# RWKV-7 mixer in a two-layer trunk: the inverse of the chunk matrices changes layout by VectorE block transposes instead of DRAM round trips, with a new order of products

## The chip, the cores and the metric

One core of one Trainium2 chip runs the whole kernel. The metric is the device time of one execution in microseconds; lower is better. The median of 3 runs of the kernel before is 1144.75 us (1141.47 to 1145.14). The core's engines are named as in the profile: PE (TensorE, with PEld for its weight loads), DVE (VectorE), ACT (ScalarE), POOL (GpSimd) and SP (SyncE, which here issues most DMAs). Everything is float32 or float32 split into two parts.

## The reference, cut to what matters

Two layers of a post-norm trunk at 256 tokens and width 1024. Each layer is SwiGLU, a mixer, SwiGLU, each followed by a layer norm. Layer 0's mixer is a chunked spatial gate; layer 1's is RWKV-7 time mixing with 16 heads of 64, and the change is in this mixer alone.

```
def step(state, inp):
    r_t, w_t, k_t, v_t, a_t, b_t = inp
    sa = jnp.einsum('bhij,bhj->bhi', state, a_t)
    state = (state * w_t[:, :, None, :] + sa[..., None] * b_t[:, :, None, :]
             + v_t[..., None] * k_t[:, :, None, :])
    y = jnp.einsum('bhij,bhj->bhi', state, r_t)
    return state, y
```

After the scan, y is normalised per head, a bonus `sum(r*k*r_k) * v` is added, the result is multiplied by a gate g and by the matrix w_o.

## The kernel before, in words

**Stages.** The 256 tokens are two row blocks of 128 (m = 0, 1), each of two chunks of 64 tokens (ch = 0 to 3). Weights stream from HBM as tiles of 128x1024 (`raw`, 4 buffers); most are split into a high part by ScalarE (line 118) and a low part by VectorE (line 119), and every product is then three matmuls (`mm3`, lines 219 to 224). R and V are multiplied natively in float32 (line 301). RWKV's scan is done in chunk form. With decays folded in (`Ep`, `Em`, and `Ex`, which is `Ep` shifted down by a row, lines 803 to 823), each chunk needs masked products of keys with queries: `ab` (line 977, the strictly lower part that must be inverted) and `scores` (`sc`, line 1003). The vectors of a chunk that replace the recurrence come from the inverse of a unit triangular 64x64 matrix for each of 16 heads and 4 chunks.

**The inverse.** Each 64x64 matrix is cut into 32x32 blocks. The 128 diagonal blocks are inverted at once on VectorE, one block per partition, its 1024 elements along the free axis: 31 steps `i0` to `i30` (line 1027), two VectorE instructions each, the second waiting for the first. To get from "row of a block per partition" to "one block per partition", `ab` stores its masked tiles to DRAM (`dA`, line 999, issued by POOL) and `inv_load` reads them back (line 1023, issued by ScalarE). On the way out `inv_out` (line 1044) stores H and a transposed copy to DRAM (`dH`, `dG`) and reads them back in two layouts, `G` and `Hf`, all issued by SP. `offdiag` (`od`) and `offdiag2` (`oe`) then make the off-diagonal block with small 32x32 matmuls, and `Hf[m]` is the finished inverse that `u` multiplies.

**The chain of chunks.** `Chunk` (line 1106) has for each chunk `av`, `x`, `rs`, `u`, `s`, `y`. `u` needs `Hf` and X; `s` needs u's result in `VU` and the gathered keys `KB` (line 885, DMAs issued by POOL); `x`, `rs` of the next chunk need the state from `s`; `y` needs `VU` and the scores. The last steps are the normalisation `on`, `og` on VectorE, the transposition `oc` and the product with w_o (`O`).

**What sets the order.** PE's and SP's instructions run in program order. For the mixer that is the string `ORDER` (line 1389), one token per step: `K h m i`, `R h m i` and `V h m i` are half-products (half h of the columns, row block m, half i of the contraction; the second half ends with `kdone`, `rdone` or `vdone`, lines 836, 899, 912), `cZ`, `cB`, `cR`, `cK` are transpositions, `lw`, `la`, `dec`, `l1_` the small low-rank products, `g1`, `g2`, `ga` the gate, `dc` the shifted Ex (line 815), `dw` the chunk decays (line 825), `p:` a parameter load. DVE, ACT and POOL are ordered by the compiler's scheduler, within the data dependences; once compiled, each runs its list in that order. Tiles named `s4` share 22 SBUF buffers, `s4x` 12, PSUM has 2 banks `mm`, 2 `tp` and 4 `acc`; a tile whose buffer is still read makes its writer wait. Weight loads are issued ahead by SP in the same queue as the other SP transfers.

**R.** `rdone` reads R's PSUM bank twice on VectorE (lines 906, 907), for R with its decay and for the bonus.

Of the kernel before, what the change touches and what calls it, by code (L numbers as in the profile page):

```python
# [22 lines left out]
P = 128  # L23
D = 1024
# [113 lines left out]
class Builder:  # L138
# [529 lines left out]
    def rwkv(self, S):  # L668

        nc = self.nc  # L670
        a = {k[5:]: v for k, v in self.a.items() if k.startswith("rwkv_")}
        V, G, A = nc.vector, nc.gpsimd, nc.scalar
        mm = nc.tensor.matmul
# [84 lines left out]
        def mix(n, m, q, out):  # L758
            for k in range(4 * q, 4 * q + 4):
                s = slice(k * P, k * P + P)  # L760
                V.scalar_tensor_tensor(out[:, s], st["xx"][m][:, s], st["mu"][:, n * 8 + k:n * 8 + k + 1],
                                       st["xf"][m][:, s], op0=ALU.mult, op1=ALU.add)
# [209 lines left out]
        def masked(out, ps, mask):  # L972
            n = mask.shape[1]
            V.tensor_tensor(out.rearrange("p (h t) -> p h t", t=n), ps.rearrange("p (h t) -> p h t", t=n),
                            mask.unsqueeze(1).broadcast_to([P, 512 // n, n]), op=ALU.mult)

        def ab(m, c):
            def f():
                if c == 0:
                    st["Aab", m] = self.s4("Aab")  # L980
                t = st["Aab", m]
# [10 lines left out]
                if c == 0:  # L992
                    return
                t3 = t.rearrange("p (b z) -> p b z", z=64)
                for blk in range(2):
                    for e in range(2):
                        b0 = blk * 64 + e * 32 + m * 16
                        r0 = e * 64 + blk * 32
# [24 lines left out]
        def inv_load():  # L1023
            st["M"] = self.s4("M")
            DI.dma_start(st["M"], self.dA.rearrange("b s t -> b (s t)"))

        def inv_step(s):
            def f():
                if s == 0:
                    st["T1"] = self.small("T1", [P, 256])  # L1030
                M3, H3 = (st[k].rearrange("p (s t) -> p s t", s=32) for k in "MH")
                n = 31 - s
                hv, tv = H3[:, 0:s + 1, s + 1:32], st["T1"][:, :(s + 1) * n].rearrange("p (s t) -> p s t", t=n)
                V.tensor_tensor(tv, H3[:, 0:s + 1, s:s + 1].broadcast_to([P, s + 1, n]),
                                M3[:, s:s + 1, s + 1:32].broadcast_to([P, s + 1, n]), op=ALU.mult)
                V.tensor_tensor(hv, hv, tv, op=ALU.add)
            return f

        def inv_zero():
            st["Hf"] = [self.s4("Hf", x=True) for m in range(2)]  # L1040
            for t in st["Hf"]:
                V.memset(t, 0.0)

        def inv_out():
            Mt, Ht = st["M"], st["H"]
            M3, H3 = (t.rearrange("p (s t) -> p s t", s=32) for t in (Mt, Ht))
            q = DO
            q.dma_start(self.dH.rearrange("b s t -> b (s t)"), Ht)
            V.tensor_copy(M3[0:64], H3[0:64].rearrange("p s t -> p t s"))
            Hf = st["Hf"]  # L1050
            q.dma_start(self.dG.rearrange("b s t -> b (s t)"), Mt[0:64, :])
            Gt = self.s4("G")
            st["G"] = Gt

            def back(m, blk, e):
                b0 = blk * 64 + e * 32 + m * 16
                r0 = e * 64 + blk * 32
                q.dma_start(
                    Hf[m].rearrange("p (b t) -> p b t", t=64)[r0:r0 + 32, :, blk * 32:blk * 32 + 32],
                    self.dH[b0:b0 + 16].rearrange("b s t -> s b t"))  # L1060

            for e in range(2):
                q.dma_start(Gt.rearrange("p (b t) -> p b t", t=32)[e * 64:e * 64 + 32],
                            self.dG[e * 32:e * 32 + 32].rearrange("b s t -> s b t"))
            for m in range(2):
                for blk in range(2):
# [200 lines left out]
        DX, DW, DA, DI, DO = A, nc.sync, G, A, nc.sync  # L1267
# [23 lines left out]
        for m in range(2):  # L1291
            ops.update({f"l1_{m}": lora1(m), f"dc{m}": decay_x(m), f"dw{m}": decay_w(m), f"kb{m}": kb(m), f"st{m}": stash(m),
                        f"un{m}": unstash(m), f"g1_{m}": lora_g1(m), f"ln{m}": ln(m), f"od{m}": offdiag(m),
                        f"oe{m}": offdiag2(m)})
            for i in range(2):
                t = f"{m}{i}"
                for n, c in ((0, "R"), (1, "K"), (2, "V"), (5, "G")):
# [3 lines left out]
                    "dec" + t: decay(m, i), "kp" + t: kprep(m, i), "zb" + t: zb(m, i), "kn" + t: kn(m, i),  # L1301
# [35 lines left out]
def body(tc, nc, stages, **a):  # L1337
    with contextlib.ExitStack() as es:
# [51 lines left out]
p:k_k cm00 cm01 l1_0 lw00 mixK00 flush mixK01 K000 K001 cm10 cm11 la00 lw01 dec00 p:k_a dec01 dc0 mixK10 p:gn_g  # L1390
l1_1 mixV00 la01 la10 lw10 mixK11 K010 kp00 K011 lw11 zb00 kp10 K100 K101 kp01 dec10 zb01 cZ00 K110 hz cB00 dw0
dec11 dc1 K111 zb10 la11 kp11 mixV01 V000 kn10 cB10 mixR00 mixG00 cB01 mixR01 V001 g1 zb11 ih kn11 kn00 cZ01 p:r_k
ab00 R000 mixG01 cZ10 R001 cZ11 cB11 ab01 cR00 mixR10 V100 ab10 ab11 iload i0 g1_0 mixG10 R100 i1 i2 i3 R101 dw1
mixV10 p:gn_b kn01 i4 cR01 i5 st0 mixG11 mixV11 V010 cK00 sc000 V011 i6 i7 i8 rs0 i9 kb1 g2 cK10 cK11 i10 i11 V101
g1_1 cK01 i12 i13 i14 sc001 V110 i15 sc010 i16 kb0 V111 i17 mixR11 i18 i19 i20 i21 i22 i23 i24 i25 st1 vu00 sc011
i26 i27 ga00 i28 i29 av0 vu01 x0 i30 iout R010 od0 od1 oe0 bo00 oe1 bo01 u0 gb R011 s0 R110 cR10 av1 vu10 x1 R111
u1 rs1 ga01 s1 cR11 sc100 y0 vu11 sc101 y1 av2 sc110 x2 rs2 u2 sc111 un0 on00 on01 og00 y2 bo10 s2 av3 ga10 og01 x3
# [21 lines left out]
```

## Time and profile before

| | before |
|---|---|
| median of 3 runs | 1144.75 us |
| the profiled execution | 1143.73 us, span 1142.0 us |
| instructions | 15347 |
| mean granted PE clock | 0.988 |
| busy share of the span: PE, PEld, DVE, ACT, POOL | 97%, 77%, 61%, 42%, 4% |
| DMA, mean over the span | 190 GB/s |
| RWKV mixer | about 724.9 to 945.7 us of the span |

Times in rows are microseconds from the span's start. A row of the timeline gives start, duration, engine, line, operation, output and inputs, and in brackets the idle time of that engine just before it with what ended it. An engine name with q (SPq, ACTq) is its queue, which issues DMAs. [...] PE's matmuls are pipelined, so a busy PE is not necessarily PE at its peak.

### The profile page before, as it was taken

Reading aid. Unit: us, or ns where it says so; the run is one execution under the profiler, and the core shown is the slowest. Engines: PE = TensorE matmul, PEld = TensorE weight load, DVE = VectorE, ACT = ScalarE, POOL = GpSimd, SP = SyncE. Lnnn points to the kernel's source line nnn. Section 1 sums busy time; section 2 is a strip of 40 time slices with the busy share of each in tenths; the row PEclk is TensorE's granted clock in tenths of the full one; section 3 lists DMA queues with packets and bytes.
Section 4 is the critical chain, followed back from the end, with each engine's and each line's share of the span. In section 5 each row is a group of like instructions: output and inputs, shape, how many; then the busy total and the mean of one; then the engine's idle time right before and its main releaser. Section 6 shows DMA issues by size and latency. Waiting matters only on the chain.

```text
span 1142.0 us, 15347 instructions
## 1 busy us (share of the span) xinstructions
PE 1103.9 (97%) x5860; PEld 879.1 (77%) x5860; DVE 698.7 (61%) x969; ACT 480.5 (42%) x636; POOL 42.2 (4%) x44
## 2 busy tenths in 40 slices
PE   8999999999999999999999999999989889999997
PEld 5888888778888788888888888775555668788885
DVE  6654556769658555457655453878655787555544
ACT  5544443455335444444444452462123245444430
POOL 0000000100000000000000000112100110000000
PEclk9999999999999999999999999999999989999999
DMA  8776565775645766655677563437876146766530
GB/s 289 236 235 185 185 197 168 232 268 196 208 148 155 240 206 198 186 183 157 197 221 225 183 202 124 166 93 256 271 203 237 43 129 191 239 204 196 184 111 38
DMA packets 153933, 216.51 MB, mean 190 GB/s; under 512 B 21213, under 2 KB 114845, under 8 KB 153858
## 3 DMA queue, kind: packets, MB, share of 16 engines
q1 hardware_dynamic: 152394, 210.80, 57.7%
q0 software_dynamic: 1024, 3.15, 1.0%
q10 hardware_dynamic: 440, 1.57, 0.4%
q8 instruction: 46, 0.75, 0.3%
q14 instruction: 29, 0.24, 0.1%
HBM read 209.46 MB, written 3.42 MB: 186 GB/s over the span
## 4 chain that ended last, share of the span: by engine, by line
PE 81%; DVE 7%; DMA 5%; issue 2%; ACT 2%; POOL 1%; ACTq 0%; SPq 0%; DVEq 0%; POOLq 0%
PE mm L221 15%; PE mm L223 15%; PE mm L222 15%; PE acc L221 8%; PE acc L222 8%; PE acc L223 8%; PE mm L301 3%; DMA raw<-ffn_w_in 2%; DVE wl L119 2%; PE tp L415 2%; POOL rs L259 1%; PE tp L235 1%; ACT wh L118 1%; DMA raw<-rwkv_w_rkv 1%; PE tp L577 1%
## 5 line engine op out<-in xcount | busy, mean ns | idle before, releaser
L119 DVE TENSOR_TENSOR wl<-raw,wh 128x1024 fp32r<-128x1024 f32 (+1 forms) x332 | 396.2, 1209 | 267.1 <-ACT wh L118 259.8
L118 ACT CAST wh<-raw 128x1024 fp32r<-128x1024 f32 (+1 forms) x332 | 340.3, 1041 | 340.8 <-PE acc L223 146.0
L221 PE MATMUL mm<-wh,xh 128*128 128x512 f32 x832 | 327.3, 393 | 5.5 <-ACT wh L118 2.4
L222 PE MATMUL mm<-wl,xh 128*128 128x512 f32 x832 | 324.7, 390 | 0.6 <-DVE wl L119 0.6
L223 PE MATMUL mm<-wh,xl 128*128 128x512 f32 x832 | 325.1, 391 | 0.2 <-DVE xl L228 0.2
L221 PEld LDWEIGHTS mm<-wh,xh 128*128 128x128 f32 x832 | 156.5, 188 | 41.5 <-ACT wh L118 3.9
L223 PEld LDWEIGHTS mm<-wh,xl 128*128 128x128 f32 x832 | 156.6, 188 | 34.6 <-DVE xl L228 1.9
L222 PEld LDWEIGHTS mm<-wl,xh 128*128 128x128 f32 x832 | 156.7, 188 | 33.1 <-DVE wl L119 1.3
L221 PE MATMUL acc<-wh,hT 128*128 128x512 f32 x352 | 141.4, 402 | 0.0
L222 PE MATMUL acc<-wl,hT 128*128 128x512 f32 x352 | 137.4, 390 | 0.0
L223 PE MATMUL acc<-wh,hT 128*128 128x512 f32 x352 | 137.4, 390 | 0.0
L404 ACT ACTIVATE h<-mm 128x256 f32<-128x256 f32 x88 | 33.8, 384 | 106.0 <-PE mm L223 105.9
L223 PEld LDWEIGHTS acc<-wh,hT 128*128 128x128 f32 x352 | 66.1, 188 | 14.8
L222 PEld LDWEIGHTS acc<-wl,hT 128*128 128x128 f32 x352 | 66.2, 188 | 12.6
L221 PEld LDWEIGHTS acc<-wh,hT 128*128 128x128 f32 x352 | 66.1, 188 | 12.7
L405 DVE TENSOR_TENSOR h<-h,mm 128x256 f32<-128x256 f32 x88 | 36.8, 418 | 59.8 <-ACT h L404 59.8
L301 PE MATMUL mm<-raw,mix 128*128 128x512 f32 x128 | 59.4, 609 | 0.9 <-DMA raw<-rwkv_w_rkv 0.9
L259 POOL TENSOR_TENSOR rs<-ve,mhalf 128x1 f32<-128x1 f32 x14 | 14.2, 1011 | 926.2 <-DVE ve L267 926.2
L301 PEld LDWEIGHTS mm<-raw,mix 128*128 128x128 f32 x128 | 23.6, 193 | 26.6 <-issue 23.8
L228 DVE TENSOR_TENSOR hT<-tp,hT 128x512 fp32r<-128x512 f32 x44 | 30.2, 686 | 7.6 <-ACT hT L227 7.6
L227 ACT CAST hT<-tp 128x512 fp32r<-128x512 f32 x44 | 25.9, 588 | 9.0 <-PE tp L415 8.9
L227 ACT CAST xh<-tp 128x512 fp32r<-128x512 f32 x24 | 13.2, 588 | 34.9 <-PE tp L235 34.9
(193 smaller groups left out, 884.2 us busy)
## 6 DMA issues: line engine op xcount, KB each, us to landing
raw<-ffn_w_in SPq DMA_DIRECT2D x352, 256.0 KB, 4.0
raw<-ffn_w_out SPq DMA_DIRECT2D x88, 512.0 KB, 4.2
raw<-rwkv_w_rkv SPq DMA_DIRECT2D x40, 512.0 KB, 3.9
raw<-sgu_w_in SPq DMA_DIRECT2D x32, 512.0 KB, 5.6
raw<-sgu_w_out SPq DMA_DIRECT2D x16, 512.0 KB, 4.3
raw<-rwkv_w_o SPq DMA_DIRECT2D x8, 512.0 KB, 3.4
lng<-ln_g SPq DMA_DIRECT2D x6, 512.0 KB, 6.0
lnb<-ln_b SPq DMA_DIRECT2D x6, 512.0 KB
```

The lines of the kernel that those rows point to most:

```text
L118: i = nc.scalar.copy(h[:, s], raw[:, s])
L119: j = nc.vector.tensor_tensor(l[:, s], raw[:, s], h[:, s].bitcast(F32), op=ALU.subtract)
L221: i = mm(out, lhsT=lh, rhs=rh, start=start, stop=False)
L222: mm(out, lhsT=lh, rhs=rl, start=False, stop=False)
L223: mm(out, lhsT=ll, rhs=rh, start=False, stop=stop)
L227: i = self.nc.scalar.copy(h, src)
L228: return i, self.nc.vector.tensor_tensor(l, src, h.bitcast(F32), op=ALU.subtract)
L259: self.nc.gpsimd.tensor_tensor(rs, v, self.mhalf[:, :w], op=ALU.pow)
L301: i = self.nc.tensor.matmul(ps, lhsT=xs[:, c], rhs=h[:, s], start=kk == 0, stop=kk == 7)
L404: nc.scalar.activation(hb[:, o + 256:o + 512], ps[:, 0:256], AF.Silu)
L405: nc.vector.tensor_tensor(hb[:, o:o + 256], hb[:, o + 256:o + 512], ps[:, 256:512], op=ALU.mult)
L415: nc.tensor.transpose(ps[:, o:o + P], st["h"][c][:, hh:hh + P], self.ident)
```

## The change

The inverse no longer uses DMAs. `ab` makes two masked tiles of 128x256 from its bank, `Aof` (columns 32 to 63 of each 64) and `D` (columns 0 to 31), and ScalarE copies the lower diagonal block from `Aof` into `D`. `inv_load` is one VectorE transpose of 32x32 blocks, `inv_out` two (`G`, `Hd`), and new steps `hf0`, `hf1` copy the diagonal blocks into `Hf`, which POOL instead of VectorE sets to zero. `od` and `oe` use `acc` banks and share their evacuations between ScalarE and VectorE. R leaves PSUM by one ScalarE copy into `rk`; its products become the steps `rm` (R times decay, in place) and `rb` (the bonus). `behind` keeps VectorE's mixing, mask, `rm`, `rb` and step instructions in written order from `i0` to the transpose of G; later ones come after that transpose. The Ex transfers (`DX`) are issued by SP instead of ScalarE. `ORDER` is new.

```diff
-                V.tensor_tensor(R[:, s], ps, st["E"][m][0][:, s], op=ALU.mult)
-                V.tensor_tensor(rk, ps, st["kp"][m][:, s], op=ALU.mult)
+                    st["rk", m] = self.s4("rk")
+                s = half(h)
+                A.copy(st["rk", m][:, s], ps)
+        def rmul(m, h):
+                behind(V.tensor_tensor(R[:, s], st["rk", m][:, s], R[:, s], op=ALU.mult))
+        def rbonus(m, h):
+                behind(V.tensor_tensor(rk, rk, st["kp"][m][:, s], op=ALU.mult))
+                V.tensor_tensor(rk, rk, st["r_k"][:, s], op=ALU.mult)
+                V.tensor_reduce(bo[:, h * 8:h * 8 + 8], heads(rk), axis=AX.X, op=ALU.add)
...
-                masked(t[:, half(c)], ps, self.mask[:, 0:64])
-                        DA.dma_start(self.dA[b0:b0 + 16].rearrange("b s t -> s b t"),
+                for out, k in ((Of, 32), (D, 0)):
+                    V.tensor_tensor(out.rearrange("p (b t) -> p b t", b=8), p3[:, :, k:k + 32],
+                                    self.mask[:, k:k + 32].unsqueeze(1).broadcast_to([P, 8, 32]), op=ALU.mult)
+                for e in range(2):
+                    r = slice(e * 64 + 32, e * 64 + 64)
+                    A.copy(D[r, :], Of[r, :])
...
-            DI.dma_start(st["M"], self.dA.rearrange("b s t -> b (s t)"))
+            V.transpose(st["M"].rearrange("p (s t) -> p t s", s=32), st["D"].rearrange("p (b t) -> p t b", b=32))
...
+        def behind(inst):
+            if st.get("step"):
+                self.after(inst, st["step"])
+                if "G" not in st:
+                    st["step"] = inst
...
-                V.memset(t, 0.0)
+                G.memset(t, 0.0)
...
+            behind(V.transpose(t.rearrange("p (b s) -> p s b", b=32), H.rearrange("p (s t) -> p s t", s=32)))
+            V.transpose(st["Hd"].rearrange("p (b t) -> p t b", b=32), H.rearrange("p (s t) -> p t s", s=32))
+        def inv_fill(m):
+                for blk in (1, 0):
+                    for e in range(2):
+                        (V.tensor_copy if m and e else A.copy)(out, src)
...
-        DX, DW, DA, DI, DO = A, nc.sync, G, A, nc.sync
+        DX, DW = nc.sync, nc.sync
```

The new order, from the first step of the mixer to the tail that is the same as before:

```
p:k_k cm00 cm01 l1_0 lw00 mixK00 flush mixK01 K000 K001 cm10 cm11 la00 lw01 dec00 p:k_a dec01 mixK10
l1_1 mixV00 la01 la10 lw10 mixK11 dc0 K010 kp00 K011 lw11 zb00 kp10 K100 st0 K101 st1 kp01 dec10 zb01 cZ00 K110 cB00 dw0
dec11 dc1 K111 zb10 la11 kp11 mixV01 V000 kn10 cB10 mixR00 mixG00 cB01 mixR01 V001 zb11 ih kn11 kn00 cZ01
ab00 R000 mixG01 cZ10 R001 cZ11 cB11 ab01 mixR10 rm00 mixR11 ab10 ab11 iload i0 i1 cR00 R100 i2 i3 cK00 i4 i5 i6
cK10 V100 i7 i8 kn01 i9 cK01 V101 i10 i11 R101 dw1 i12 i13 i14 hz R010 i15 i16 rm01 cR01 i17 i18 i19 i20 sc000 R011 i21 i22 i23
cK11 i24 i25 rs0 kb1 R110 i26 i27 i28 i29 i30 iout vu00 od0 od1 hf0 sc001 oe0 oe1 hf1 p:r_k g1 g2 sc010 av0 x0 R111 u0 sc011 kb0
mixV10 s0 g1_0 mixV11 vu01 mixG10 av1 x1 rs1 V010 u1 mixG11 V011 s1 rm10 cR10 rm11 p:gn_b V110 y0 p:gn_g cR11 sc100 y1 V111 rb00 rb01 sc101 vu10 av2 x2 rs2
gb g1_1 bo00 bo01 u2 vu11 ga00 on00 on01 sc110 ga01 s2 sc111 rb10 rb11 un0 og00 y2 bo10 av3 og01 x3 ga10
rs3 u3 ga11 bo11 y3 oc00 O00 O10 on10 on11 oc01 O20 un1 og10 O30 og11 xw O40 O50 O60 O70 oc10 ln0 oc11 O01 O11 O21
```

## Rows read from the trace of the kernel before

**Rows 1.** The page, part 1: busy time, share of the span, instructions of PE.
```profile
PE 1103.9 (97%) x5860; PEld 879.1 (77%) x5860; DVE 698.7 (61%) x969; ACT 480.5 (42%) x636; POOL 42.2 (4%) x44
```

**Rows 2.** Busy time by stretch: engine busy (count), then granted clock, DMA share, GB/s.
```profile
724.90:799.20 74.30, 70.34 (x405) 47.19 (x403) 60.27 (x134) 34.04 (x59) 11.99 (x10) 0.98 0.57 190
799.20:849.50 50.30, 44.92 (x220) 24.72 (x220) 34.31 (x87) 9.44 (x22) 5.67 (x10) 1.00 0.79 248
849.50:864.40 14.90, 13.35 (x296) 10.05 (x296) 3.60 (x6) 3.93 (x6) 0.00 (x0) 0.66 0.64 185
864.40:882.60 18.20, 16.90 (x221) 10.38 (x220) 12.14 (x16) 7.09 (x9) 0.00 (x0) 1.00 0.70 244
882.60:914.30 31.70, 26.92 (x489) 22.25 (x489) 22.50 (x40) 7.60 (x12) 3.61 (x2) 1.00 0.17 59
914.30:945.70 31.40, 26.91 (x114) 21.42 (x113) 28.15 (x42) 12.72 (x15) 5.05 (x3) 0.89 0.45 137
...
747.60:752.30 4.70, 4.68 (x11) 2.89 (x12) 3.79 (x12) 3.88 (x6) 0.00 (x0) 0.67 0.08 24
```

**Rows 3.** PE's waits by releaser: us in total, times, longest.
```profile
PE tp L1013 <- DVE VU L1160: 1.6, 1, 1.6
...
PE tp L1079 <- DMA G<-dG: 1.5, 2, 1.2
PE acc L799 <- ACT ah L790: 1.5, 1, 1.5
...
PE tp L235 <- DVE a L875: 1.2, 1, 1.2
...
PE tp L1191 <- ACT gs L1189: 0.8, 2, 0.4
```

**Rows 4.** Timeline of ScalarE and its queue, then of PE, 743 to 778 us.
```profile
743.44 1.33 ACTq L821 DMA_DIRECT2D Ex<-Ep  x1
...
746.51 0.62 ACT L227 CAST mh<-mix 128x512 fp32r<-128x512 f32 x1 [2.61 <-DMA Ex<-Ep]
...
777.36 0.59 ACT L842 COPY kp<-mm 128x512 f32<-128x512 f32 x1 [6.97 <-DMA Ex<-Ep]
...
747.62 1.12 PE L799 MATMUL acc<-a,ah 65*128 65x512 f32 x2 [1.49 <-ACT ah L790]
```

**Rows 5.** VectorE by line, 811.9 to 839.0 us: busy, mean ns | idle before.
```profile
L1036 DVE TENSOR_TENSOR H<-H,T 128x31 f32<-128x31 f32 (+15 forms) x31 | 10.6, 343 | 1.0
L1034 DVE TENSOR_TENSOR T<-H,M 128x31 f32<-128x31 f32 (+15 forms) x31 | 10.6, 342 | 1.0
...
L1049 DVE COPY M<-H 64x1024 f32<-64x1024 f32 x1 | 1.1, 1055 | 0.0
```

**Rows 6.** Durations: timeline rows of PE and VectorE, and the page's part 5.
```profile
802.33 7.03 PE L301 MATMUL mm<-raw,mix 128*128 128x512 f32 x16
...
820.23 1.04 PE L235 MATMUL tp<-ident,Em 128*128 128x128 f32 x8
...
885.96 1.16 PE L1013 MATMUL tp<-ZR,KBT 64*128 64x128 f32 x16
...
901.15 1.29 DVE L974 TENSOR_TENSOR A<-tp,mask 128x512 f32<-128x512 f32 x2
...
L119 DVE TENSOR_TENSOR wl<-raw,wh 128x1024 fp32r<-128x1024 f32 (+1 forms) x332 | 396.2, 1209 | 267.1 <-ACT wh L118 259.8
```

**Rows 7.** Timeline of SP's queue at the inverse's end.
```profile
840.08 0.42 SPq L1048 DMA_DIRECT2D dH<-H  x1
...
847.12 0.96 SPq L1063 DMA_DIRECT2D G<-dG  x2
```

**Rows 8.** POOL's timeline; DMA issues: count, KB each, median us to landing.
```profile
827.53 0.51 POOL L890 DMA_DIRECT2D KB<-Em  x1 [13.67 <-PE tp L1186]
...
dX<-x POOLq DMA_DIRECT2D x2, 512.0 KB, 3.5
...
KB<-a POOLq DMA_DIRECT2D x3, 256.0 KB, 6.4
```

More of the change, by code (lines that the diff above doesn't have):

```diff
@@ L760, in mix @@
                 s = slice(k * P, k * P + P)
-                V.scalar_tensor_tensor(out[:, s], st["xx"][m][:, s], st["mu"][:, n * 8 + k:n * 8 + k + 1],
-                                       st["xf"][m][:, s], op0=ALU.mult, op1=ALU.add)
+                behind(V.scalar_tensor_tensor(out[:, s], st["xx"][m][:, s], st["mu"][:, n * 8 + k:n * 8 + k + 1],
+                                              st["xf"][m][:, s], op0=ALU.mult, op1=ALU.add))
         def mix_in(n, m, q):
@@ L902, in f @@
                     st["R"][m] = (st["E"][m][0], self.small(f"bonus{m}", [P, NH]))
-                R, bo = st["R"][m]
-                rk = self.s4("rk")[:, 0:512]
-                s = slice(h * 512, h * 512 + 512)
-                V.tensor_tensor(R[:, s], ps, st["E"][m][0][:, s], op=ALU.mult)
-                V.tensor_tensor(rk, ps, st["kp"][m][:, s], op=ALU.mult)
+                    st["rk", m] = self.s4("rk")
+                s = half(h)
+                A.copy(st["rk", m][:, s], ps)
+            return f
+        def rmul(m, h):
+            def f():
+                R, s = st["R"][m][0], half(h)
+                behind(V.tensor_tensor(R[:, s], st["rk", m][:, s], R[:, s], op=ALU.mult))
+            return f
+        def rbonus(m, h):
+            def f():
+                s = half(h)
+                rk, bo = st["rk", m][:, s], st["R"][m][1]
+                behind(V.tensor_tensor(rk, rk, st["kp"][m][:, s], op=ALU.mult))
                 V.tensor_tensor(rk, rk, st["r_k"][:, s], op=ALU.mult)
@@ L973, in masked @@
             n = mask.shape[1]
-            V.tensor_tensor(out.rearrange("p (h t) -> p h t", t=n), ps.rearrange("p (h t) -> p h t", t=n),
-                            mask.unsqueeze(1).broadcast_to([P, 512 // n, n]), op=ALU.mult)
+            behind(V.tensor_tensor(out.rearrange("p (h t) -> p h t", t=n), ps.rearrange("p (h t) -> p h t", t=n),
+                                   mask.unsqueeze(1).broadcast_to([P, 512 // n, n]), op=ALU.mult))
         def ab(m, c):
             def f():
-                if c == 0:
-                    st["Aab", m] = self.s4("Aab")
-                t = st["Aab", m]
+                if c == 0 and m == 0:
+                    st["D"], st["Aof"] = self.s4("D"), self.s4("Aof")
+                b0 = (m * 16 + c * 8) * 32
+                D, Of = (st[k][:, b0:b0 + 256] for k in ("D", "Aof"))
                 ps = self.tpb()
@@ L990, in f @@
                            tile_position=(e * 64, e * 64))
-                masked(t[:, half(c)], ps, self.mask[:, 0:64])
[L992 to L998, printed above, removed]
-                        DA.dma_start(self.dA[b0:b0 + 16].rearrange("b s t -> s b t"),
-                                    t3[r0:r0 + 32, :, blk * 32:blk * 32 + 32])
+                p3 = ps.rearrange("p (b t) -> p b t", b=8)
+                for out, k in ((Of, 32), (D, 0)):
[4 more added lines that the diff above has]
+                    A.copy(D[r, :], Of[r, :])
             return f
@@ L1033, in f @@
                 hv, tv = H3[:, 0:s + 1, s + 1:32], st["T1"][:, :(s + 1) * n].rearrange("p (s t) -> p s t", t=n)
-                V.tensor_tensor(tv, H3[:, 0:s + 1, s:s + 1].broadcast_to([P, s + 1, n]),
-                                M3[:, s:s + 1, s + 1:32].broadcast_to([P, s + 1, n]), op=ALU.mult)
-                V.tensor_tensor(hv, hv, tv, op=ALU.add)
-            return f
+                behind(V.tensor_tensor(tv, H3[:, 0:s + 1, s:s + 1].broadcast_to([P, s + 1, n]),
+                                       M3[:, s:s + 1, s + 1:32].broadcast_to([P, s + 1, n]), op=ALU.mult))
+                st["step"] = V.tensor_tensor(hv, hv, tv, op=ALU.add)
+            return f
+        def behind(inst):
[3 more added lines that the diff above has]
+                    st["step"] = inst
         def inv_zero():
@@ L1041, in inv_zero, with f @@
             for t in st["Hf"]:
-                V.memset(t, 0.0)
+                G.memset(t, 0.0)
         def inv_out():
[L1045 to L1066, printed above, removed]
-                    for e in range(2):
-                        back(m, 1 - blk, e)
+            H = st["H"]
+            t = self.s4("G")
+            behind(V.transpose(t.rearrange("p (b s) -> p s b", b=32), H.rearrange("p (s t) -> p s t", s=32)))
+            st["G"] = t
+            st["Hd"] = self.s4("Hd")
+            V.transpose(st["Hd"].rearrange("p (b t) -> p t b", b=32), H.rearrange("p (s t) -> p t s", s=32))
+        def inv_fill(m):
+            def f():
+                for blk in (1, 0):
+                    for e in range(2):
+                        r = slice(e * 64 + blk * 32, e * 64 + blk * 32 + 32)
+                        out = st["Hf"][m].rearrange("p (b t) -> p b t", t=64)[r, :, blk * 32:blk * 32 + 32]
+                        src = st["Hd"][r, m * 512:m * 512 + 512].rearrange("p (b t) -> p b t", t=32)
+                        (V.tensor_copy if m and e else A.copy)(out, src)
+            return f
         def offdiag(m):
@@ L1083, in f @@
                     q0 = e * 64 + 32
-                    A.copy(Q[q0:q0 + 32, m * 512:m * 512 + 512], ps[q0:q0 + 32, :])
+                    (A.copy if e else V.tensor_copy)(Q[q0:q0 + 32, m * 512:m * 512 + 512], ps[q0:q0 + 32, :])
             return f
@@ L1098, in f @@
                     d0 = e * 64
-                    V.tensor_copy(st["Hf"][m].rearrange("p (b t) -> p b t", t=64)[d0:d0 + 32, :, 32:64],
-                                  ps[d0:d0 + 32, :].rearrange("p (b t) -> p b t", t=32))
+                    (A.copy if e else V.tensor_copy)(
+                        st["Hf"][m].rearrange("p (b t) -> p b t", t=64)[d0:d0 + 32, :, 32:64],
+                        ps[d0:d0 + 32, :].rearrange("p (b t) -> p b t", t=32))
             return f
@@ L1389 @@
 ORDER = """
[L1390 to L1397, printed above, removed]
+p:k_k cm00 cm01 l1_0 lw00 mixK00 flush mixK01 K000 K001 cm10 cm11 la00 lw01 dec00 p:k_a dec01 mixK10
[6 more added lines that the diff above has]
+gb g1_1 bo00 bo01 u2 vu11 ga00 on00 on01 sc110 ga01 s2 sc111 rb10 rb11 un0 og00 y2 bo10 av3 og01 x3 ga10
 rs3 u3 ga11 bo11 y3 oc00 O00 O10 on10 on11 oc01 O20 un1 og10 O30 og11 xw O40 O50 O60 O70 oc10 ln0 oc11 O01 O11 O21
```

15 lines of the change are left out of this document (6 added, 9 removed).

## The prediction

> **What bounds the kernel now.** I read the page's busy shares first: PE is busy 1103.9 of 1142.0 us [rows 1], so an edit pays or costs only where PE idles or runs at a low clock. Next the busy time by stretch, over the RWKV mixer alone, the only part that the change touches [rows 2]. From the mixer's first transposes (724.9) to the next layer's (945.7), PE idles (stretch minus busy) 4.0 us up to the last product for the inverse (`ab11`, 799.2), 5.4 to the start of `od0` (849.5), then 1.6 and 1.3 through chunk 0 and chunk 1, 4.8 through chunks 2 and 3 (to 914.3), and 4.5 in the output projection: 21.5 us together. [...] Third, PE's waits by releaser [rows 3]: nothing dominates; each is under 2 us, and the order after `y3` is not edited. So this is a sum of small terms. The profiled execution took 1143.73 us with a span of 1142.0; it is 1.0 us under the median 1144.75 of runs that spread from 1141.47 to 1145.14. I sum against 1143.73. About 0.3% (3.4 us) is what a measurement can tell from no change.
>
> **Ex leaves ScalarE's queue.** Before, ScalarE issues the four Ex transfers of half m=0 from 743.44 on, and its next instruction runs at 746.51 after 2.61 us idle; PE meanwhile needs `ah` and starts `la10` 1.49 us late [rows 4]. In the 4.7 us after that wait the clock is 0.67 [rows 2], which loses 4.7 x 0.33 = 1.55 us. On SP the same issues (some 3 us, 743.44 to 746.51) stand behind weight loads already issued, and nothing asks for Ex before `zb00`, which comes after two K half-products and `kp00`. Both terms go: -1.5 and -1.55. What is late next is `mixK11`'s split, which runs on the freed ScalarE.
>
> [...]
>
> For m=1 ScalarE idles 6.97 us ahead of `kp` at 777.36 [rows 4]. The four issues are some 3 of it; for the other 4 I see only one reason, that Ex waits for a buffer of the 22-slot ring. Counting tiles through both orders, the old one wants up to 26 there (two fewer once the stashes have run), the new one some 22, since `Aab`, `r_k`, `gn_g` and the `g1` tiles no longer precede it. The two memsets of `Hf` also leave VectorE. Of the 1.2 us wait for `a` [rows 3] I take off 0.8. On SP dc1 stands behind two dW round trips and ahead of the next weight loads; no row of the old order shows that price, so it goes to the list of what could prove me wrong.
>
> **Into the inverse.** `V100` and `cR00` move behind `ab11`, so it ends 3.9 us of PE work earlier; no saving by itself. The two masked products per `ab` (128x256 for one of 128x512) and ScalarE's two copies put D some 2.0 us behind `ab11`; a transpose follows. No row shows a transpose. The nearest is the strided copy of 1024 elements per partition, 1.055 us [rows 5]; I take 1.1, bounded by half of that (a faster mode) and twice (two passes). The steps then start 3.2 us behind `ab11`. They cost 10.6 + 10.6 us plus 2.0 of gaps [rows 5] = 23.2. Written among them are `rm01` (0.6) and the masks of `sc000` (1.3, [rows 6]), held in this order; G's transpose adds 1.1. VectorE is done at 3.2 + 23.2 + 0.6 + 1.3 + 1.1 = 29.4 us, and 30.3 with 0.9 waiting for `sc000`.
>
> PE has seven native half-products in that time (16 matmuls take 7.03 and the last one's end overlaps what follows, so 8 take 3.45): 24.2, six groups of four transposes at 0.5 (eight in 1.04) and one `sc` at 1.16 [rows 6]: 28.3 us. `od0` then waits 2.0 us. Before it waited 1.5 for G from DRAM [rows 3], so this wait is replaced, not removed. With slow transposes it is 4.1, with fast ones 1.4.
>
> **Out of it.** Before, H leaves at 840.08 and G's return is issued at 847.12 [rows 7], with the eight transfers for Hf behind it in the queue; PE covers that with products and still idles. Now G, Hd, the Q copies and `hf` stay on VectorE and ScalarE, and `sc001`, `sc010` and `R111` cover them. I keep the slow clock of this passage as it was: `od` and `oe` are the same small matmuls.
>
> **R by ScalarE, new order.** R's copy (0.6 us as the cast in [rows 4], four times) frees its bank sooner; the products run on SBUF. Nothing on PE waits for them but `cR`. For the rest I walked PE through the new list by hand with the durations above and the two `tp` banks, each freed by its reader. Waits left: 0.8 for the two `gs`; 0.6 ahead of `sc000`; 2.0 at `od0`; 1.5 in `sc011` behind u0's bank, the pattern of the 1.6 row [rows 3]; 0.8 at s0 behind masks; 0.5 at `sc100`; 1.4 at `av2`, since nothing stands between `sc101` and it; 0.7 each at `sc110` and `ga01`; 0.8 at `sc111`: 9.8. The old idle between 799.2 and 914.3 is 13.0 [rows 2], so -3.2. In this walk u0 starts 46 us behind `ab11`, s0 50, V010 58, `V111` ends at 80 and `y3` at 112; the old list takes 115.1 (799.2 to 914.3), 119.0 with the 3.9 that move into it. Of that difference I count only the 3.2 of idle: a walk at full clock without gaps flatters the new list. Against it: the `rb` work, `bo00`, `bo01` and four weight splits move into the last two chunks, where VectorE is now busy 22.5 of 31.7 [rows 2]; I add 1.2 us for two evacuations that come late.
>
> **Sum.** -1.5 - 1.55 - 0.8 - 3.2 + 1.2 = -5.85; 1143.73 - 5.85 = 1137.9, so **1138**. The tail keeps its 4.5 us of idle. Removed DMAs are otherwise costed at nothing: they ran beside PE's products.
>
> **Rivals.** *Larger gain:* VectorE reaches `iout` before PE runs dry (2.0 back), half the clock's loss in its passage (14.9 x 0.34 = 5.1, so 2.5) does not recur, and a bank wait vanishes (1.1): 1138 - 5.6, about 1132. For it: fewer idle ends around `od`. Against: `od0` still has a VectorE chain ahead.
>
> *KB late:* `kb0` is now last before s0. By my walk s0 comes 50 us behind `ab11`. If the slot is one that `sc011` frees at 49, two issues of 0.5 and a landing of 6.4 [rows 8] make s0 some 6.5 us late, and 1138 becomes 1144.5. For it: before, these transfers also sat 13.67 us waiting for a slot. Against: by my count one slot is free from `hf1` on (40), and then it lands at 47, 3 us early. [...]
>
> *Slow transposes:* twice the price adds 2.1 at `od0` and up to 2 on Hd and the clock: 1142.
>
> *VectorE full in the last two chunks (slower):* from `cR11` to `y3` its work grows from 22.5 by four `rb` (1.9 each), two `bo` (2.5) and three more splits (1.2 each, [rows 6]) to 36.3 us, in some 41. Ten evacuations that PE waits for (four pairs of masks, two VU, two X, two S) then queue behind whole `rb` groups. If each loses 1.2 us, 12 us go and the saving of 7.05 with it: about 1149. It eats the saving from 0.7 us each and is slower by the bound from 1.05. For it: VectorE takes its instructions in one fixed order, and after G that order is not written by hand. Against: nothing in `rb` is due before `bo`.
>
> *The change does not do what it says:* an instruction that sets the order on VectorE costs no time of its own, so this is only that the waits come back elsewhere; it is in the two rivals near no change.
>
> **How the numbers follow.** Forecast (1134.5 to 1141.3) 0.50; larger gain 0.20; KB late 0.12 and slow transposes 0.06, both within 0.3%; VectorE full 0.12. So faster 0.70, same 0.18, slower 0.12. The range leaves out the far end of the larger gain and the slower rival: 1129 to 1146.
>
> **What would show it.** Right: PE's row for `ah` gone and the clock at 747 full; transposes near 1.1 us; steps starting about 3 us behind `ab11`; `od0` waiting about 2 us; waits named A and VU under `tp` banks. Wrong: s0 waiting for KB; a transpose of 2 us or more; VectorE above 90% busy before `y3` with PE waits on it longer than 1 us; weights late, as SP now also issues Ex.

## The result and the profile after

The changed kernel takes 1150.05 us (median of 4 runs, 1149.45 to 1150.66) beside 1143.95 for the kernel before: 1.0056 times as long, 95% interval 1.0037 to 1.0075. It is 6.1 us slower, where 5.85 us faster was predicted.

The kernel after, busy time by stretch, in the columns of [rows 2]: from the second half of the mixer's first LoRA product (its 16 matmuls with `xx`) to the end of `ab11`, to the start of `od0`, to `u0`, to the end of `y3`.

```profile
728.20:791.40 63.20, 61.41 (x370) 41.76 (x368) 51.11 (x116) 34.69 (x61) 12.18 (x10) 1.00 0.51 170
791.40:822.90 31.50, 28.68 (x99) 14.26 (x99) 27.74 (x71) 7.98 (x18) 0.00 (x0) 1.00 0.74 230
822.90:841.00 18.10, 16.78 (x328) 12.70 (x329) 13.19 (x20) 7.54 (x12) 2.04 (x4) 0.62 0.61 190
841.00:921.50 80.50, 68.85 (x814) 49.87 (x814) 41.80 (x75) 19.67 (x32) 3.29 (x2) 0.89 0.38 131
```

The kernel before, cut at the same events:

```profile
728.10:799.10 71.00, 67.38 (x382) 44.48 (x380) 57.14 (x128) 32.96 (x57) 11.99 (x10) 0.98 0.55 183
799.10:849.60 50.50, 44.95 (x221) 24.77 (x222) 34.51 (x88) 9.44 (x22) 5.67 (x10) 1.00 0.79 248
849.60:856.80 7.20, 6.49 (x256) 6.18 (x256) 1.44 (x3) 2.31 (x4) 0.00 (x0) 0.64 0.74 165
856.80:914.40 57.60, 50.75 (x751) 36.54 (x750) 36.80 (x58) 16.32 (x22) 3.61 (x2) 0.96 0.39 137
```

Up to `ab11` the change wins 7.8 us; 3.9 of that is PE work moved behind it, 3.9 is gain. From `ab11` to `y3` it takes 130.1 us, where before it took 115.3, or 119.2 with the moved work: 10.9 us lost. PE's idle time behind `ab11` went from 13.1 to 15.8 us (stretch minus busy). The clock weighs more: lost clock (stretch times one minus the granted clock) was 2.6 + 2.3 = 4.9 us before and is 6.9 + 8.9 = 15.8 after. Idle and clock together make 2.7 + 10.9 = 13.6 more, above the 10.9 because idle time inside a slow stretch is in both. Behind `y3` some 1.4 us come back.

In slices of 1 us the granted clock reads 1.00 or 0.50 in both kernels, and a value between only in a slice where it changes; over a longer stretch it is a mean of the two. Where PE's clock falls in the kernel after (same columns; every slow stretch stands behind the stretch with the gap):

```profile
820.00:825.00 5.00, 2.74 (x130) 2.10 (x128) 4.83 (x7) 0.27 (x1) 0.00 (x0) 1.00 0.82 263
825.00:840.00 15.00, 13.68 (x204) 10.44 (x199) 11.12 (x19) 7.27 (x12) 2.04 (x4) 0.54 0.60 181
840.00:845.00 5.00, 3.72 (x51) 2.46 (x49) 3.83 (x11) 1.16 (x2) 0.00 (x0) 1.00 0.60 208
845.00:855.00 10.00, 7.89 (x91) 7.32 (x93) 5.97 (x15) 0.72 (x3) 0.00 (x0) 0.66 0.01 2
880.00:885.00 5.00, 3.44 (x36) 1.90 (x34) 3.04 (x4) 2.76 (x4) 0.00 (x0) 1.00 0.75 259
885.00:895.00 10.00, 9.18 (x132) 7.65 (x133) 4.12 (x8) 2.92 (x6) 0.00 (x0) 0.83 0.65 248
900.00:905.00 5.00, 2.51 (x36) 1.42 (x36) 3.15 (x6) 0.59 (x1) 2.23 (x2) 0.90 0.01 3
905.00:912.00 7.00, 6.23 (x75) 5.94 (x78) 7.00 (x13) 0.00 (x0) 0.00 (x0) 0.58 0.00 0
```

In such a stretch PE counts as busy while its matmuls take longer (16 of them 4.48 us in place of 2.44, below). That is why PE's busy time over the whole span rose from 1103.9 [rows 1] to 1108.9 us for the same work. PE's waits from `ab11` to `y3`, in the columns of [rows 3]:

```profile
PE tp L1176 <- DVE A L985: 2.9, 2, 1.7
PE acc L1089 <- DVE G L1065: 2.3, 1, 2.3
PE tp L1023 <- DVE S L1182: 2.2, 1, 2.2
PE tp L1023 <- ACT ZR L964: 1.8, 2, 1.5
PE mm L1140 <- ACT VU L934: 1.5, 1, 1.5
PE acc L1104 <- issue: 1.3, 1, 1.3
PE tp L1023 <- DVE VU L1171: 1.3, 1, 1.3
```

And the transposes, with two PE rows of the second slow stretch:

```profile
793.91 2.04 DVE L1035 STREAM_TRANSPOSE M<-D 128x1024 f32<-128x1024 f32 x1 [1.67 <-ACT D L1010]
820.91 1.90 DVE L1065 STREAM_TRANSPOSE G<-H 128x1024 f32<-128x1024 f32 x1
...
846.72 1.97 PE L1176 MATMUL tp<-VU,KB 128*64 128x64 f32 x32 [1.74 <-DVE A L985]
848.62 4.48 PE L1197 MATMUL tp<-g,mix 128*128 128x160 f32 x16
```

`s0` (L1176) waits 1.74 us for a mask, and `g1_0` (L1197) behind it takes 4.48 us; the same 16 matmuls take 2.44 at the full clock, in the kernel before and in the runs with fills. KB is not the releaser.

### The profile page after: what moved, and what is told of

The parts are those of the page before. It is cut to its first block, busy times and chain, and to the rows that moved or that the text cites. A ratio compares the mean times of both kernels' runs of the same rounds, so it can differ in the third digit from the quotient of the medians.

```text
span 1147.7 us, 15343 instructions
## 1 busy us (share of the span) xinstructions
PE 1108.9 (97%) x5860; PEld 884.2 (77%) x5860; DVE 702.4 (61%) x975; ACT 489.2 (43%) x654; POOL 38.1 (3%) x38
## 4 chain that ended last, share of the span: by engine, by line
PE 81%; DVE 9%; DMA 4%; ACT 2%; issue 2%; POOL 1%; SPq 0%; DVEq 0%; ACTq 0%; POOLq 0%
PE mm L221 15%; PE mm L223 15%; PE mm L222 15%; PE acc L221 8%; PE acc L222 8%; PE acc L223 8%; DMA raw<-ffn_w_in 2%; PE mm L301 2%; DVE wl L119 2%; PE tp L415 2%; POOL rs L259 1%; PE tp L235 1%; ACT wh L118 1%; DVE H L1046 1%; DVE T L1044 1%
```

## The experiments

Times are medians; a ratio is to the kernel before on the same chip, with its 95% interval. "Behind l1" counts from the second half of the first LoRA product (728.1 before, 728.2 after), which takes out what differs ahead of the mixer.

**Matmuls whose results nobody uses, in PE's waits.** They do no useful work, so they help only by what PE does in place of idling. Theory C puts the loss in the low clock behind PE's waits (0.54 from 825 to 840, above): the one fill at `od0` would win 5 to 6.5 us back, to about 1144. Theory W puts it in the waits alone.

```diff
                 ps = self.accb()
+                for _ in range(14 - 14 * m):
+                    mm(ps[:, 0:P], lhsT=self.ident, rhs=self.ident, start=True, stop=True)
```

> One edit to the changed kernel: 14 matmuls of 128x128 (results unused, into the bank that od0 then overwrites; about 1.6 us at the full clock) go on TensorE ahead of od0, inside its 2.26 us wait for G. [...] Theory W (waits alone): the 1.6 us were idle anyway, VectorE and ScalarE set the pace behind od0, and the time stays within 1 us of 1150.

Measured: 1151.74 us, 1.0051 (1.0034 to 1.0069): no gain. The wait at `od0` is gone, but PE then waits 0.7 + 0.7 us for the Q copies, and the slow stretch only begins later (1.00 up to 830, 0.66 from 830 to 840). From `od0` to `u0` the clock is 0.71 in place of 0.62:

```profile
826.50:844.40 17.90, 16.45 (x330) 11.75 (x328) 13.11 (x21) 7.63 (x12) 2.02 (x4) 0.71 0.66 200
```

The 14 matmuls took 3.2 us, not the 1.6 expected, so `od0` came 0.7 us after G was ready. Theory C in its narrow form, one wait that costs 6 us, fell.

The other waits get theirs as steps of their own, `Fsc011` ahead of `sc011` and so on (for `sc011`, `s0` and `sc100` into a free `acc` bank, else into an `mm` bank):

```diff
+        def fill(n, bank):
+            def f():
+                ps = bank()
+                for _ in range(n):
+                    mm(ps[:, 0:P], lhsT=self.ident, rhs=self.ident, start=True, stop=True)
+            return f
```

> As the fill ahead of od0, and the same matmuls also ahead of sc011 (8), s0 (10), sc100 (10), av2 (8), ga01 (4), s2 (6) and sc111 (12), each sized under the wait that the trace shows there. Theory C: all four slow stretches of the changed kernel (lost clock 6.9 + 3.4 + 1.8 + 3.4 = 15.4 us, from the granted clock of their windows, against 5.1 before) shrink, and the time falls to 1139 to 1142. Theory W: no change, 1149 to 1151, or slower by what the fills overrun. If only the first stretch recovers, about 1144.

Measured: 1145.88 us, 1.0005 (0.9990 to 1.0020): some 6 us back, short of theory C's 1139 to 1142. Three of the four slow stretches are gone; the one around `oe` stays.

The same loop with `range(6)` in `offdiag2`:

> The kernel with all fills, plus 6 more of the same matmuls ahead of oe0 and of oe1, inside their waits of 0.69 and 0.76 us for the Q copies; with these TensorE has no gap over 0.4 us from 819 to 840. If a low clock follows waits alone, the last slow stretch (829 to 836 at 0.50) goes as well and 3 us more are saved: 1142 to 1143.5. If the 32x32 matmuls of od and oe lower the clock by themselves, the granted clock is 0.50 again within 10 us of od0 and the time stays at 1145 to 1147.

Measured: 1143.42 us, 0.9968 (0.9954 to 0.9981). From `od0` to `u0` and from `u0` to `y3`, first with the fills without `oe`; then with them, where the first line begins at the end of `ab11`:

```profile
822.20:838.50 16.30, 14.81 (x331) 11.12 (x330) 13.10 (x21) 7.63 (x12) 2.02 (x4) 0.79 0.69 197
838.50:915.30 76.80, 74.93 (x930) 56.25 (x930) 41.35 (x74) 19.67 (x32) 3.29 (x2) 1.00 0.41 137
```

```profile
791.90:824.30 32.40, 31.87 (x124) 17.44 (x124) 28.61 (x71) 7.98 (x18) 0.00 (x0) 1.00 0.73 227
824.30:838.90 14.60, 14.60 (x355) 11.67 (x354) 13.04 (x21) 7.64 (x12) 2.03 (x4) 1.00 0.65 199
838.90:915.70 76.80, 74.92 (x930) 56.24 (x930) 41.37 (x74) 19.79 (x32) 3.29 (x2) 1.00 0.43 143
```

With all gaps filled the granted clock is 1.00 from `ab11` to `y3`, with the same 32x32 matmuls in `od` and `oe`; so these do not lower the clock by themselves. By the ratios 1.0056 and 0.9968 this is 0.9% or 10 us. In the profiled executions `ab11` to `y3` takes 130.1 us in the changed kernel, 125.4 with the first fills and 123.8 with all: 6.3 of the 10.9 us lost come back, although the fill at `od0` ran past its wait by 0.7 us. Behind `y3`, where no fill stands, the execution with all fills is 2.2 us longer, so that over the whole only 4.1 us are left (419.5 and 415.4 us behind l1). The loss is thus mostly clock, and it follows the waits; its size lies between 6 and 10 us, and what the rest is was not separated.

**The order of products.** In the first new order `R111` goes ahead of `od0`, `sc011` ahead of `u0`, and a native product between most steps of the state chain:

```diff
-cK11 i24 i25 rs0 kb1 R110 i26 i27 i28 i29 i30 iout vu00 od0 od1 hf0 sc001 oe0 oe1 hf1 p:r_k g1 g2 sc010 av0 x0 R111 u0 sc011 kb0
-mixV10 s0 g1_0 mixV11 vu01 mixG10 av1 x1 rs1 V010 u1 mixG11 V011 s1 rm10 cR10 rm11 p:gn_b V110 y0 p:gn_g cR11 sc100 y1 V111 rb00 rb01 sc101 vu10 av2 x2 rs2
-gb g1_1 bo00 bo01 u2 vu11 ga00 on00 on01 sc110 ga01 s2 sc111 rb10 rb11 un0 og00 y2 bo10 av3 og01 x3 ga10
+cK11 i24 i25 rs0 kb1 R110 mixV10 i26 i27 i28 i29 i30 iout vu00 R111 od0 od1 hf0 sc001 oe0 oe1 hf1 p:r_k g1 g2 sc010 av0 x0 sc011 kb0
+mixV11 V010 u0 vu01 mixG10 av1 V011 s0 g1_0 mixG11 rm10 rm11 x1 rs1 cR10 cR11 u1 rb00 V110 s1 rb01 p:gn_b y0 p:gn_g sc100 V111 vu10 y1 sc101
+av2 x2 sc110 rs2 gb g1_1 u2 vu11 ga00 s2 bo00 bo01 sc111 on00 on01 y2 un0 av3 og00 x3 ga01 og01 rb10 rb11 ga10 bo10
```

> The changed kernel with another product order behind ab11: R111 ahead of od0 instead of behind x0, sc011 ahead of u0, V010, V011, V110, V111 and g1 each between two steps of the state chain, rb and on put where VectorE idles. No work added or dropped. Theory C: od0 no longer waits, the clock stays at 1.00 from 820 to 840, and the time is 1136 to 1141. Theory W or a full VectorE: the waits come back at the masks and at the state, and it stays at 1146 or more.

Measured: 1138.89 us, 0.9944 (0.9922 to 0.9967), faster than both kernels with every new part of the change in it. From `ab11` to `y3` it takes 116.0 us, 14 less than the change's own list. The stretch around `oe` is still slow (0.50 from 830 to 840), and a short one behind the wait at `av2` (0.66 from 875 to 880); from `u0` to `y3` the clock is 0.97 all the same:

```profile
844.20:905.80 61.60, 57.43 (x790) 41.52 (x790) 34.44 (x60) 19.08 (x31) 3.27 (x2) 0.97 0.46 154
```

The third new order changes the end of that list, and holds the group norm back on VectorE (`mk` is the last mask written so far, `xadd` the last addition to X):

```diff
-s1 rb01 p:gn_b
+s1 rb01 rb10 rb11 p:gn_b
...
-av2 x2 sc110 rs2 gb g1_1 u2 vu11 ga00 s2 bo00 bo01 sc111 on00 on01 y2 un0 av3 og00 x3 ga01 og01 rb10 rb11 ga10 bo10
+rs2 av2 x2 vu11 sc110 bo00 bo01 bo10 bo11 gb g1_1 u2 ga00 s2 sc111 y2 un0 av3 x3 on00 on01 ga01 og00 og01 ga10
-rs3 u3 ga11 bo11 y3
+rs3 u3 ga11 y3
...
-                V.tensor_tensor(yn, Y, per_head(s1, 8), op=ALU.subtract)
+                self.after(V.tensor_tensor(yn, Y, per_head(s1, 8), op=ALU.subtract), st["mk"])
...
-                V.tensor_tensor(yn, yn, per_head(rs, 8), op=ALU.mult)
+                self.after(V.tensor_tensor(yn, yn, per_head(rs, 8), op=ALU.mult), st["xadd"])
```

> The first new product order with rs2 ahead of av2, the bonus work (bo) moved to where VectorE idles behind sc110, and the group norm of the first half held behind sc111's masks and the X of chunk 3. If waits are what is left to win, av2's wait for VU (1.56 us), y2's for VU (1.11) and part of the 4.8 us in the output projection (wl, xl, o) go: 1134 to 1137. If VectorE's total work sets the end of the projection, it stays at 1138 to 1139.

Measured: 1133.40 us, 0.9888 (0.9867 to 0.9909), just below the range, and the fastest here without useless matmuls. `av2` waits 0.8 in place of 1.6 us and the wait of `y2` is gone; in the projection the waits for `wl`, `xl` and `o` (2.2 + 1.3 + 1.7) became one for `o` of 3.8. What is left up to `y3`: the two largest of PE's waits there, then the clock from `od0` to `u0` and from `u0` to `y3`:

```profile
PE acc L1104 <- issue: 3.0, 1, 3.0
PE tp L1023 <- issue: 1.6, 1, 1.6
```

```profile
822.80:845.00 22.20, 17.58 (x345) 13.43 (x344) 17.87 (x30) 8.12 (x13) 2.03 (x4) 0.69 0.64 189
845.00:903.90 58.90, 55.84 (x790) 40.13 (x790) 36.31 (x62) 19.18 (x31) 3.27 (x2) 1.00 0.48 161
```

From the first new order, one product moved:

```diff
-hf0 sc001 oe0 oe1 hf1 p:r_k g1 g2 sc010 av0 x0 sc011 kb0
-mixV11 V010 u0
+mixV11 hf0 sc001 oe0 V010 oe1 hf1 p:r_k g1 g2 sc010 av0 x0 sc011 kb0
+u0
```

> The new product order of the fill experiment with one more move: V010 goes between oe0 and oe1 (and mixV11 ahead of hf0), so that the run of small matmuls is broken by a native half-product that also covers the Q copies. If the waits between od and oe make the clock fall at 827, it stays near 1.00 to 845 and the time is 1133 to 1136. If the small matmuls themselves do it, the granted clock still falls to 0.5 within 10 us of od0 and the time stays at 1137 to 1141.

Measured: 1148.00 us, 1.0017 (1.0001 to 1.0033). The time didn't answer its question, because moving `V010` put two more weight loads ahead of r_k in SP's queue (38 in place of 36), and these waited until `V010` itself had read their buffers; r_k was issued at 838.6 us in place of 823.1. VectorE then sat on a bonus product, with the masks behind it, and `u0` waited 7.8 us:

```profile
848.57 1.29 DVE L919 TENSOR_TENSOR rk<-rk,r_k 128x512 f32<-128x512 f32 x2 [6.98 <-DMA r_k<-rwkv_r_k]
...
850.61 1.97 PE L1166 MATMUL tp<-X,Hf 64*64 64x64 f32 x32 [7.81 <-DVE A L985]
```

The clock did fall to 0.50 (830 to 835), as the second theory had it, but behind a stop of PE of 1.4 us; so this run doesn't tell the two apart.

**The stop without a releaser.** The third new order with the loop of 6 matmuls in `offdiag2`:

> The third new order with 6 matmuls of 128x128 ahead of oe0 and 6 ahead of oe1. In the third order TensorE stops 3.0 us inside oe1 and 1.6 us inside an sc for no releaser that the trace shows, and 14 us at a low clock lie around it. Theory I (instructions arrive too slowly for a run of 32x32 matmuls): wide matmuls between them give time, the stops go, the clock stays near 1.00 from 825 to 845 and the time falls by 5 to 8 us, to 1126 to 1129. Rival (the stop has another cause, as the load of the queues by r_k and g): the stop stays over 2 us and the time at 1131 to 1134.

Measured: 1130.96 us, 0.9905 (0.9869 to 0.9940). The clock stays at 1.00 from 820 to 845, but PE still stops 2.0 us in `oe` and 0.8 in an `sc`. It ran on another chip than the run without the fill, and the two ratios (0.9888, 0.9905) don't tell them apart; the time is at the edge of the rival's range, with theory I's clock.

And with real work there:

```diff
-hf0 sc001 oe0 oe1 hf1 p:r_k g1 g2 sc010 av0
+hf0 sc001 oe0 sc010 oe1 hf1 p:r_k g1 g2 av0
```

> The same with real work in that place: sc010 goes between oe0 and oe1. Theory I: 16 matmuls of 64x128 are narrow too and give about 1 us; the stop is shorter, not gone: 1130 to 1134. If only the wait for Q counts, the clock stays up and it is 1127 to 1130. If sc010 waits there for the masks of sc001, a wait of 0.5 to 1.5 us appears and it is 1134 to 1137.

Measured: 1133.87 us, 0.9910 (0.9889 to 0.9930): no gain; stops of 2.4 and 1.0 us, the clock at 0.5 behind them.

Where the stops lie says more than these times. First the third order, then this run:

```profile
827.74 0.37 PE L1023 MATMUL tp<-ZR,KBT 64*128 64x128 f32 x1 [1.62 <-issue]
828.05 2.89 PE L1104 MATMUL acc<-Hd,Q 32*32 32x32 f32 x127
833.94 0.26 PE L1104 MATMUL acc<-Hd,Q 32*32 32x32 f32 x1 [3.00 <-issue]
```

```profile
829.46 0.37 PE L1023 MATMUL tp<-ZR,KBT 64*128 64x128 f32 x1 [2.36 <-issue]
829.77 1.73 PE L1104 MATMUL acc<-Hd,Q 32*32 32x32 f32 x64
831.43 2.08 PE L1023 MATMUL tp<-ZR,KBT 64*128 64x128 f32 x16
833.43 1.48 PE L1104 MATMUL acc<-Hd,Q 32*32 32x32 f32 x47
835.93 0.68 PE L1104 MATMUL acc<-Hd,Q 32*32 32x32 f32 x17 [1.02 <-issue]
```

Between the two stops lie 1 + 127 and 1 + 64 + 16 + 47 matmuls: 128 each time, with 128 weight loads, whatever the products are. With the fill it is 1 + 12 + 64 + 12 + 39, again 128. So the place of a stop goes by the count of PE's instructions and not by a product or by r_k and g. Why a stop is long in one run and absent in another stays open.

**Parts of the change.** The changed kernel with the old `ORDER`, in which only these steps are new or moved, and so for the other halves of R (besides r_k's load and `rb00`, `rb01` to behind `hf1`, and gn_g's load to ahead of `og00`):

```diff
-R001 cZ11
+R001 rm00 cZ11
...
-od0 od1 oe0 bo00 oe1 bo01 u0 gb R011 s0 R110 cR10
+od0 od1 hf0 oe0 oe1 hf1 p:r_k rb00 bo00 rb01 bo01 u0 gb R011 rm10 rb10 s0 R110 cR10
```

> The changed kernel's new parts (transposes, ScalarE for R, VectorE in written order, Ex on SP) with the product order of the kernel before; only rb, hf and three parameter loads are placed so that it can run. Theory C (the new product order makes the waits and so the slow clock): the stretch from ab11 to y3 is back near the old 115 us and the time is 1139 to 1144. Rival M (the new parts themselves cost: transposes of 2 us, VectorE held to one order): 1147 or more, with TensorE waiting for VectorE in the steps and at the masks.

Measured: 1152.75 us, 1.0061 (1.0040 to 1.0082): rival M. VectorE, held to its list, does the masks of `sc011` only after steps that the old list puts ahead of them, and `ga00` waits for their bank:

```profile
PE tp L1217 <- DVE A L985: 5.0, 1, 5.0
```

The same, with the hold switched off, and then the changed kernel with this one edit:

```diff
-            if st.get("step"):
+            if False:
```

> The old product order with the new parts, as before, but VectorE not held to the written order among the steps. If holding the order is what made ga00 wait 5.0 us for the masks of sc011, that wait shrinks under 2 us and the time falls from 1152.8 to 1143 to 1147. If the new parts cost elsewhere, it stays above 1150.

Measured: 1148.37 us, 1.0023 (1.0006 to 1.0041), just above the range; the wait is 0.8. PE now stops 3.5 us in `u0` without a releaser and waits 2.8 for a weight load and 2.8 for R, and from `ab11` to `y3` it takes 124.8 us against 115.3 before. So the old list doesn't carry the new parts either: each was a list written for its own waits.

> The changed kernel with one part undone: VectorE is not held to the written order among the steps. If the written order is what makes the new list work (as its author's list supposes), G comes later than 820.9 by the work that gets in between, od0 waits longer and the time is above 1150. If the held order costs (as it did in the old product order), it falls to 1145 to 1148.

Measured: 1152.15 us, 1.0045 (1.0030 to 1.0060), no difference from the change that can be measured; `od0` waits 2.8 in place of 2.3 us.

For Ex the edit is one name, the issuing engine: back to ScalarE in the changed kernel, to SP in the one before:

```diff
-        DX, DW = nc.sync, nc.sync
+        DX, DW = A, nc.sync
```

> The changed kernel with one part undone: ScalarE issues Ex's transfers again. If Ex on SP is worth what the prediction gave it (3.05 us for ah and the clock behind it, up to 0.8 more for the wait for a), ab11 ends 3 to 4 us later and the time goes from 1150 to about 1153. Rival (issue time is small, or the steps of the inverse wait for something else anyway): within 1 us of 1150.

Measured: 1154.81 us, 1.0069 (1.0054 to 1.0083), which overlaps the change's own interval. In the profiled execution `ab11` ends 68.9 us behind l1 in place of 63.2 and `y3` 199.7 in place of 193.3: in the changed kernel the part is worth 5.7 us at `ab11`, while the time alone is inconclusive.

> The kernel before with this one part alone: SP issues Ex's transfers instead of ScalarE. If the part stands on its own, TensorE's wait for ah and the low clock at 747 go and the time is 3 us under the kernel before (ratio about 0.997). Rival (given back: the head ends earlier but the inverse's DMA chain or the weight loads behind Ex on SP hold it): ratio 0.999 to 1.003.

Measured: 1147.97 us, 1.0029 (1.0013 to 1.0045): slower, as the rival had it. The row for `ah` is gone, and in its place stand

```profile
PE mm L222 <- DVE wl L119: 2.9, 1, 2.9
PE tp L235 <- DVE a L875: 2.3, 1, 2.3
```

And with gn_g's load out of the head too:

```diff
-k_a dec01 dc0 mixK10 p:gn_g
+k_a dec01 dc0 mixK10
...
-og00 y2
+p:gn_g og00 y2
```

> The kernel before with Ex on SP, as in the run that came out at 1.0029, and one more edit: the load of gn_g goes from the head to just before og00. Theory S (slots: the load held a slot of the 22 and stood in the queue ahead of the weights, so the wait for ah came back as one for wl): V000 starts 40.4 us behind the first product of the LoRA group as in the changed kernel (43.7 in the kernel before), and the ratio is 0.996 to 0.999. Rival (the head's gain is given back later in the inverse whatever the head does): ratio 1.000 to 1.004.

Measured: 1145.27 us, 1.0008 (0.9992 to 1.0024). Theory S's landmark is there, `V000` at 40.4 us, but `ab11` ends 71.2 us behind l1, as in the kernel before (71.0): `a` still costs 2.3 us. The head's gain exists only with the change's other moves there (earlier stashes, parameter loads and `g1` out of the head, Hf's memset on GpSimd); which of them it needs was not separated.

**The price of a transpose.**

```diff
-            V.transpose(st["M"].rearrange("p (s t) -> p t s", s=32), st["D"].rearrange("p (b t) -> p t b", b=32))
+            V.transpose(st["M"], st["D"])
```

> The changed kernel with M's transpose reading and writing contiguous rows (its blocks then lie in another layout, so the inverse computes something else) and G's transpose split into two of 512 elements; Hd's as it is. If the stride of the access sets the price, M falls from 2.04 to about 1.1 us; if the transpose itself does, M stays at 1.9 to 2.0 and the halves of G take about half of 1.90 each, plus a fixed part.

A single execution, 1149.01 us. Busy us, mean ns:

```profile
L1072 DVE STREAM_TRANSPOSE Hd<-H 128x1024 f32<-128x1024 f32 x1 | 2.0, 2008 | 0.0
L1067 DVE STREAM_TRANSPOSE G<-H 128x512 f32<-128x512 f32 x2 | 1.9, 1024 | 0.0
L1035 DVE STREAM_TRANSPOSE M<-D 128x1024 f32<-128x1024 f32 x1 | 1.2, 1245 | 1.7 <-ACT D L1010 1.7
```

The stride sets most of the price: 1.25 us contiguous, 2.0 strided, and half the elements take half the time.

## Why the prediction was wrong

**The term that failed** is the -3.2 us "of idle" behind `ab11`, with the sentence "I keep the slow clock of this passage as it was" and no price for the clock elsewhere. The text said that "a walk at full clock without gaps flatters the new list", and then charged only idle time. With the 1.2 us for late evacuations the sum had 2.0 us won behind `ab11`; measured are 10.9 us lost. Behind the new list's waits, of 2.3 us at most, the granted clock is 0.50 in four places (826 to 839, 846 to 852, 887 to 890 and 905 to 910), for 15.8 us of lost clock against 4.9. With the waits filled by useless matmuls the granted clock is 1.00 from `ab11` to `y3` and the kernel is faster than the one before: shown by the pair of fills. Had only two of the walk's waits been charged with a stretch like the one in [rows 2] (14.9 us at 0.66, 5.1 lost), the sign would have turned. Its own rows also hold a third slow passage that it didn't name, the output projection (0.89 over 31.4 us, 3.5 lost); there the change did no harm (0.94 over 30.9 us).

**The idle itself** was undersized too: 9.8 us foreseen, 15.8 measured (2.8 + 1.3 + 11.7). `sc011`, `av2`, `ga01` and the two `gs` came within 0.3 us of the walk. Missed were 1.3 inside `oe`, 0.9 more at `s0`, 1.0 more at `sc100` (its ZR copy stands behind a weight cast on ScalarE), 1.1 at `s2` and 1.35 more at `sc111`.

**The head** was right in size: 3.05 + 0.8 foreseen, 3.9 measured, 3.3 of it by `V000`; `ah`'s row is gone, the clock is full. That the small term fits is partly luck: the wait of 1.2 for `a` is gone, but one of 1.0 for `kk` has come later on. The reason given was too simple, since Ex on SP alone is worth nothing measurable in the kernel before, and 5.7 us at `ab11` in the changed one.

**Into the inverse**: PE's 28.3 us came as 28.7, VectorE's 30.3 as 31.4, `od0`'s wait of 2.0 as 2.26. The transposes took 2.04, 1.90 and 1.96 us, the rival's price. That VectorE's sum came out so near is luck: the steps began 4.6 us behind `ab11` in place of 3.2 and G's transpose took 0.8 more, but the 0.9 us foreseen for `sc000` was never waited. Filling `od0`'s wait bought nothing.

**The rivals.** "VectorE full" named 1149, almost the time that came, by a mechanism that did not decide: from 875 to 921.5 VectorE is busy 28.3 of 46.5 us, and the fills win the loss back without taking any work off it. Queueing behind whole groups does show in `sc111` and `s2`, but the groups there are the norm and the bonus sum, not `rb`. KB's four transfers were issued from 832.3 to 834.6 and took 3.8 to 4.6 us to land, where the rival had 6.4, in time for `s0` at 846.7. What R's way through ScalarE is worth by itself was not tried.

## What to carry to other kernels

When an order of products is changed, price each wait of TensorE twice: its length, and the stretch at a granted clock of 0.50 that can follow (3 to 14 us each in the changed kernel); here the two came to the same size over the passage (15.8 us each). A cheap test tells the two apart: put matmuls of unused result into the waits, and what the time wins is clock (a little less than the clock costs, where a fill outlasts its wait). Then put real products there, one wide one between every two links of a serial chain, and check that the move does not drag the loads of other tiles behind its weights.

## What the runs showed that was not expected

- A 32x32 transpose of 128x1024 fp32 on VectorE takes 1.9 to 2.1 us with a strided side and 1.25 us contiguous. The same 1024 elements per lane take 1.6 times as long strided (2.04 us beside 1.25).
- TensorE stops at fixed places of its instruction list. In 13 of the 17 traces there are 20 stops with no releaser, of 0.2 to 3.5 us, in the kernel before (0.4 + 0.8) as in the changed one (1.3). Counted in matmuls, weight loads and PE's semaphore instructions, all of them stand at instruction 7873, 8129 or 8385, within one; these are 256 apart. In the three fills of the changed order and in the transpose run the same places pass without a stop. That late instructions are the cause, as theory I has it, no trace shows.
- A gap need not cost the clock: before, PE was busy 6.7 of 10 us from 895 to 905 and the granted clock stayed 1.00; in the third order with fills it stayed 1.00 over the stop of 2.0 us.
